# Low parts of weight tiles in a hybrid decoder layer: ScalarE and an accumulating DMA in place of VectorE

## Chip, cores and metric

The kernel runs on one core of one Trainium2 chip. The metric is the device time of one execution in microseconds (us); lower is better. A core has TensorE (matmuls; PE), VectorE (DVE), ScalarE (ACT), GpSimd (POOL) and SyncE (SP), each with a queue of its own that it works through in order, and 16 DMA engines that all queues share.

## What is computed

The reference is one decoder layer over 512 tokens of width 1024 in float32, with a final norm:

```python
u = rmsnorm(x, ln1_g)
q, k, v, pool_in, z, xbc, dt_raw, gate_pre = split(u @ w_in)
y_a = dilated_attention(q, k, v) @ w_a        # 3 groups of 6 heads
y_b = pool_mixer(pool_in, pool_w) @ w_b       # windows 2, 4, 8, 16
y_c = ssd(z, conv(xbc), dt_raw) @ w_c         # chunked scan, 4 chunks of 128
x = x + (sigmoid(gate_pre) * (y_a, y_b, y_c)).sum() @ w_o
x = x + (silu(conv(u2 @ w_up)[:2816]) * conv(u2 @ w_up)[2816:]) @ w_down
out = rmsnorm(x)
```

## The kernel before

**Matmuls in three products.** Each large matrix product is made of operands in a rounded 32-bit format (`F32R`). Both sides are split into a high part (the value rounded to F32R) and a low part (the value minus its high part), and `mm3` (L215 to L222) adds up three products in PSUM: high weight by high activation, high weight by low activation, low weight by high activation, in this order. So the low part of a weight tile is first read after two thirds of a chunk's matmuls.

**Weight tiles as jobs.** The weights pass through 94 jobs, one for each tile; most tiles are 1 MB (128 partitions x 2048 values). A job has three buffers to fill: `raw` (pool `wraw`, two buffers) by a DMA on SP's queue (`fetch`, L168 to L175), `wh` (three buffers) by a rounding copy on ScalarE (`cast`, L177 to L195, two halves of a tile, one for each step), and `wl` (two buffers) by a subtraction on VectorE (`low`, L197 to L210, one instruction for a tile). The loop at L1274 walks through the jobs. Ahead of the matmuls of job n it calls `prepare` (L1281 to L1292): the low part of tile n+1, the high part of tile n+2, the fetch of tile n+3. The fetch needs the raw buffer that the low part of tile n+1 has just finished with.

**The order of the work.** The order on PE, ACT, DVE and POOL is the order in which the program is written (L104); SP's order is chosen by the scheduler. A job of two 128-row chunks calls `step` after each chunk (L143), which first emits one deferred piece of work (`second`, emptied by `flush`, L137) and then one stage of each running side task: attention heads, state-space chunks, norms. Pieces that are left when a job ends are all emitted before the next one begins (L1278).

**Stages.** In order of time: projection to the pooling branch (8 chunks; POOL does its shifted sums, L621 to L643), gates, pooling output, w_b, then for three attention groups v, q and k; the convolution input xbc; the state-space chunks (`ssd_item`, L759) beside the third group and the first gates; z and the last gates; the combination of the three attention groups (`combine`, L576: POOL multiplies attention outputs by weights that SP loads); w_a, w_c, w_o (8 jobs of half the usual number of matmuls, L936), up-projection (22 jobs, `up_evac` L998), down-projection (12 jobs), final norm. Activations and side tasks use one pool of 2 KB tiles (`big`, `NBIG` = 54 buffers, L98 and L1305), handed out in rotation.

Of the kernel before, what the change touches and what calls it, by code (L numbers as in the profile page):

```python
# [11 lines left out]
F32R = mybir.dt.float32r  # L12
AF = mybir.ActivationFunctionType
OP = mybir.AluOpType
AX = mybir.AxisListType

P = 128
# [64 lines left out]
def trunk(ctx: ExitStack, tc, out, x, rel_bias, ln1_g, w_in, b_gate, w_a, pool_w, pool_scale, w_b,  # L82
# [3 lines left out]
    act, dve, pool, pe, sp = nc.scalar, nc.vector, nc.gpsimd, nc.tensor, nc.sync  # L86
# [6 lines left out]
    rows = ctx.enter_context(tc.tile_pool(name="rows", bufs=1))  # L93
    wraw = ctx.enter_context(tc.tile_pool(name="wraw", bufs=2))
    whp = ctx.enter_context(tc.tile_pool(name="whp", bufs=3))
    wlp = ctx.enter_context(tc.tile_pool(name="wlp", bufs=2))
    upool = ctx.enter_context(tc.tile_pool(name="upool", bufs=1))
    big = ctx.enter_context(tc.tile_pool(name="big", bufs=NBIG))  # L98
    ypool = ctx.enter_context(tc.tile_pool(name="ypool", bufs=2))
# [35 lines left out]
    second = []  # L135

    def flush():  # L137
        todo = second[:]
        second.clear()
        for f in todo:  # L140
            f()
# [26 lines left out]
    def fetch(job, cuts=1):  # L168
        raw = job.raw = wraw.tile([P, job.k, job.c], F32, name="raw", tag="raw")
        at = 0  # L170
        for src in job.parts:
            n = src.shape[-1] // cuts
            for i in range(cuts):
                sp.dma_start(raw[:, :, at:at + n], src[:, :, i * n:(i + 1) * n])
                at += n  # L175

    def cast(job, cuts=1, spread=False):  # L177

        w = job.c // cuts
        job.high = whp.tile([P, job.k, job.c], F32R, name="wh", tag="wh")  # L180

        def high(i):
            o = slice(i * w, (i + 1) * w)
            act.copy(job.high[:, :, o], job.raw[:, :, o])  # L184

        def at(i):
            high(i)
            if i + 1 < cuts:
                second.append(lambda: at(i + 1))

        if spread:
            second.append(lambda: at(0))
            return
        for i in range(cuts):
            high(i)  # L195

    def lows(job, cuts=1, eng=None):  # L197

        w, h = job.c // cuts, job.high
        l = wlp.tile([P, job.k, job.c], F32R, name="wl", tag="wl")  # L200
        job.split = h, l
        for i in range(cuts):
            o = slice(i * w, (i + 1) * w)
            (eng or dve).tensor_tensor(l[:, :, o], job.raw[:, :, o], h[:, :, o].bitcast(F32),  # L204
                                       OP.subtract)
            yield

    def low(job, cuts=1, eng=None):
        for _ in lows(job, cuts, eng):
            pass  # L210
# [926 lines left out]
    weights = [j for j in jobs if isinstance(j, Job)]  # L1137
# [87 lines left out]
    pe.transpose(first[2][:, :KD], g8[:KD, :P], eye[:KD, :KD])  # L1225
    dve.tensor_copy(g1, first[2][:, :KD])
    cast(weights[0], 2)
    low(weights[0], 2, pool)
    for k in range(KD):
        turn_scale(1, k % 2 * 4 + k // 2)  # L1230
    for k in range(KD):
        turned(k, 0, bank(k))
    cast(weights[1], 2)
    parts = lows(weights[1], 2)

# [28 lines left out]
    fetch(weights[3])  # L1264
    begin(0, 256, S)
    cast(weights[2])
    low(weights[2])
    begin(1, 256, S)
# [4 lines left out]
    n = 0  # L1273
    for job in jobs:  # L1274
        if not isinstance(job, Job):
            job.fn()
            continue
        while second:  # L1278
            flush()
        if n >= 2:  # L1280
            def prepare(n=n, later=False):  # L1281

                def rest():
                    if n + 1 < len(weights):
                        low(weights[n + 1])
                    if n + 2 < len(weights):
                        cast(weights[n + 2], 2, spread=not later)
                    if n + 3 < len(weights):
                        fetch(weights[n + 3])
                if later:  # L1290
                    return rest
                rest()  # L1292

            if job.late:
                job.prepare = prepare
            else:
                prepare()
            job.body(job.split)
        n += 1
# [2 lines left out]

# [1 line left out]
ORDERED = {EngineType.PE, EngineType.Activation, EngineType.DVE, EngineType.Pool}  # L1304
NBIG = 54  # L1305
MIX = "ZZ0zz1ggggaa"
SSD_ORDER = ((0, 0, 1), (1, 0, 1), (0, 1, 1), (2, 0, 1), (1, 1, 1), (3, 0, 1), (2, 1, 1), (3, 1, 1))
WARM = 12
# [29 lines left out]
```

## Time and profile before

| | us |
|---|---|
| median of 3 runs (1057.33 to 1058.59) | 1057.51 |
| profiled execution, its own time | 1058.24 |
| span of that profile | 1056.4 |
| TensorE busy | 1044.1 |
| VectorE busy, of it L204 (low parts) | 576.7, 219.2 |
| ScalarE busy, of it L184 (high parts) | 430.9, 187.2 |
| GpSimd busy | 134.9 |

The share of busy time is an average over all stages. The DMA engines are busy for 35.9% of the span with the traffic of SP's queue, and move 109 GB/s in the mean. The 1.8 us between the span and the execution's own time lie around the span.

### The profile page before, as it was taken

Reading aid. Unit: us, or ns where it says so; the run is one execution under the profiler, and the core shown is the slowest. Engines: PE = TensorE matmul, PEld = TensorE weight load, DVE = VectorE, ACT = ScalarE, POOL = GpSimd, SP = SyncE. Lnnn points to the kernel's source line nnn. Section 1 sums busy time; section 2 is a strip of 40 time slices with the busy share of each in tenths; the row PEclk is TensorE's granted clock in tenths of the full one; section 3 lists DMA queues with packets and bytes.
Section 4 is the critical chain, followed back from the end, with each engine's and each line's share of the span. In section 5 each row is a group of like instructions: output and inputs, shape, how many; then the busy total and the mean of one; then the engine's idle time right before and its main releaser. Section 6 shows DMA issues by size and latency. Waiting matters only on the chain.

```text
span 1056.4 us, 13018 instructions
## 1 busy us (share of the span) xinstructions
PE 1044.1 (99%) x5268; PEld 872.5 (83%) x5268; DVE 576.7 (55%) x777; ACT 430.9 (41%) x698; POOL 134.9 (13%) x118
## 2 busy tenths in 40 slices
PE   8999999999999999999999999999999999999997
PEld 8878889898788887787888888898888888888885
DVE  5552523245667538576658756766556565532315
ACT  6343412232545633567555323554444434431311
POOL 1580000000000001100143500002111111110100
PEclk9999999999999999999999999999999999999999
DMA  7236233242221355542252426542322323232312
GB/s 241 77 116 180 80 102 94 86 124 67 83 80 60 81 152 137 150 126 57 69 150 83 157 80 217 184 141 80 117 83 94 105 81 120 80 120 77 103 60 80
DMA packets 116426, 115.50 MB, mean 109 GB/s; under 512 B 5235, under 2 KB 101302, under 8 KB 116367
## 3 DMA queue, kind: packets, MB, share of 16 engines
q1 hardware_dynamic: 116367, 114.68, 35.9%
q8 instruction: 41, 0.67, 0.3%
q14 instruction: 18, 0.15, 0.0%
HBM read 110.87 MB, written 2.22 MB: 107 GB/s over the span
## 4 chain that ended last, share of the span: by engine, by line
PE 91%; DMA 2%; issue 2%; ACT 1%; DVE 1%; SPq 1%; POOL 0%; DVEq 0%; ACTq 0%; POOLq 0%
PE pa L221 35%; PE pu L221 22%; PE pb L221 19%; PE pqk L221 7%; DMA al<-ad 1%; PE ps L512 1%; PE pu L1036 1%; PE ppw L221 1%; PE po L551 1%; PE pt L539 1%; DVE wl L204 1%; DMA raw<-in_w_in_dram 1%; SPq L468 1%; PE py L808 1%; PE pyo L814 1%
## 5 line engine op out<-in xcount | busy, mean ns | idle before, releaser
L204 DVE TENSOR_TENSOR wl<-raw,wh 128x2048 fp32r<-128x2048 f32 (+3 forms) x94 | 219.2, 2333 | 137.9 <-PE pb L221 67.6
L184 ACT CAST wh<-raw 128x1024 fp32r<-128x1024 f32 (+2 forms) x186 | 187.2, 1025 | 104.4 <-PE pb L221 41.0
L221 PE MATMUL pa<-uh,wh 128*128 128x512 f32 x384 | 99.3, 400 | 0.3 <-ACT wh L184 0.3
L1003 DVE SCALAR_TENSOR_TENSOR hc<-pu,fcol,hc 128x510 f32<-128x510 f32 x88 | 65.9, 749 | 54.5 <-ACT hc L1000 52.8
L221 PE MATMUL pa<-ul,wh 128*128 128x512 f32 x384 | 95.0, 389 | 0.0
L221 PE MATMUL pa<-uh,wl 128*128 128x512 f32 x384 | 94.9, 389 | 0.0
L221 PEld LDWEIGHTS pa<-ul,wh 128*128 128x128 f32 x384 | 72.1, 188 | 15.3
L221 PEld LDWEIGHTS pa<-uh,wl 128*128 128x128 f32 x384 | 72.1, 188 | 14.9
L221 PE MATMUL pu<-uh,wh 128*128 128x512 f32 (+1 forms) x352 | 83.7, 380 | 0.0
L221 PEld LDWEIGHTS pa<-uh,wh 128*128 128x128 f32 x384 | 69.9, 188 | 16.5 <-issue 1.7
L221 PE MATMUL pu<-ul,wh 128*128 128x512 f32 (+1 forms) x352 | 83.5, 379 | 0.0
L221 PE MATMUL pu<-uh,wl 128*128 128x512 f32 (+1 forms) x352 | 83.5, 379 | 0.0
L221 PEld LDWEIGHTS pu<-ul,wh 128*128 128x128 f32 x352 | 64.2, 188 | 12.5
L221 PEld LDWEIGHTS pu<-uh,wl 128*128 128x128 f32 x352 | 64.2, 188 | 12.4
L221 PEld LDWEIGHTS pu<-uh,wh 128*128 128x128 f32 x352 | 64.1, 188 | 12.5
L1000 ACT ACTIVATE hc<-pu,fcol,fcol 128x512 f32<-128x512 f32 x40 | 31.2, 780 | 82.1 <-PE pu L221 82.1
L1008 POOL TENSOR_TENSOR hc<-hc 128x512 f32<-128x512 f32 x22 | 31.5, 1433 | 223.3 <-DVE hc L1003 188.2
L787 POOL TENSOR_TENSOR xd<-xc,dec 128x512 f32<-128x512 f32 x6 | 6.4, 1063 | 362.9 <-DVE xc L778 344.3
L533 ACT ACTIVATE sb<-sb,nm 128x128 f32<-128x128 f32 (+1 forms) x72 | 30.1, 419 | 47.0 <-DVE nm L530 33.3
L221 PE MATMUL pb<-wh,fl 128*128 128x512 f32 x176 | 47.7, 389 | 0.0
L221 PE MATMUL pb<-wl,fh 128*128 128x512 f32 x176 | 47.7, 389 | 0.0
L221 PE MATMUL pb<-wh,fh 128*128 128x512 f32 x176 | 47.7, 389 | 0.0
(273 smaller groups left out, 1597.6 us busy)
## 6 DMA issues: line engine op xcount, KB each, us to landing
raw<-in_w_in_dram SPq DMA_DIRECT2D x25, 1024.0 KB
raw<-in_ffn_w_up_dram SPq DMA_DIRECT2D x22, 1024.0 KB
raw<-in_w_in_dram SPq DMA_DIRECT2D x20, 512.0 KB
raw<-in_ffn_w_down_dram SPq DMA_DIRECT2D x10, 1024.0 KB
raw<-in_w_o_dram SPq DMA_DIRECT2D x8, 1024.0 KB
raw<-in_w_in_dram SPq DMA_DIRECT2D x6, 768.0 KB
raw<-in_w_b_dram SPq DMA_DIRECT2D x4, 1024.0 KB
al<-ad SPq DMA_DIRECT2D x16, 256.0 KB
```

The costliest lines, as they stand in the source:

```text
L184: act.copy(job.high[:, :, o], job.raw[:, :, o])
L204: (eng or dve).tensor_tensor(l[:, :, o], job.raw[:, :, o], h[:, :, o].bitcast(F32), OP.subtract)
L221: pe.matmul(ps, l, r, start=first and n == 0, stop=last and n == total - 1)
L468: sp.dma_start(V[g, n][32 * tb:32 * tb + 32, :384], t[n:P:4, :384])
L512: pe.matmul(pss[i][:, o:o + w * P], q[r, n * P:(n + 1) * P], k[r, kb * P:(kb + w) * P], start=True, stop=True)
L533: act.activation(sb[:, off:off + w * P], sb[:, off:off + w * P], AF.Exp, bias=nm[:, n, h:h + 1], accum_out=ls[:, n, h:h + 1])
L539: pe.transpose(pt[:, o:o + P], sb[:, o:o + P], eye)
L551: pe.matmul(po[DH * hh:DH * hh + DH, n * P:(n + 1) * P], V[g, kb + i][:, (2 * c + hh) * DH:(2 * c + hh + 1) * DH], probs[2 * c + hh, nb][: ...
L808: pe.matmul(py[DH * i:DH * i + DH, j * P:(j + 1) * P], xc[:, o:o + DH], als[j // 2][:, lo:lo + P], start=True, stop=True)
L1000: act.activation(t, ps, AF.Identity, bias=ff["c1"][:, ff["b"] + m:ff["b"] + m + 1], scale=fw(2, m))
L1003: dve.scalar_tensor_tensor(t[:, sh:], ps[:, :S - sh], fw(k, m), t[:, sh:], OP.mult, OP.add)
L1008: pool.tensor_tensor(a, a, t, OP.mult)
```

## The change

Tiles 4 to 93 get their low part in another way; tiles 0 to 3 keep the old one. The new function `divide` makes four ScalarE pieces: two halves of the high part as before, and two halves of `wl`, written as the raw value times -1 and rounded to F32R, which is the negative of the high part. A DMA on POOL's queue then adds the whole raw tile to `wl` in place. `prepare` calls it for tile n+2 at job n (the low part was made for tile n+1). `wl` gets a third buffer, and the pool of 2 KB tiles shrinks from 54 to 50. Below line 194 the changed kernel's lines are 28 higher than those used here.

```diff
-    wlp = ctx.enter_context(tc.tile_pool(name="wlp", bufs=2))
+    wlp = ctx.enter_context(tc.tile_pool(name="wlp", bufs=3))
...
+    def divide(job, spread=False):
+        w = job.c // 2
+        h = whp.tile([P, job.k, job.c], F32R, name="wh", tag="wh")
+        l = wlp.tile([P, job.k, job.c], F32R, name="wl", tag="wl")
+        job.split = h, l
+        o = [slice(i * w, (i + 1) * w) for i in range(2)]
+        def add():
+            act.mul(l[:, :, o[1]], job.raw[:, :, o[1]], -1.0)
+            pool.dma_start(l, job.raw, accum_op=OP.add)
+        pieces = [lambda: act.copy(h[:, :, o[0]], job.raw[:, :, o[0]]),
+                  lambda: act.copy(h[:, :, o[1]], job.raw[:, :, o[1]]),
+                  lambda: act.mul(l[:, :, o[0]], job.raw[:, :, o[0]], -1.0), add]
+        def at(i):
+            pieces[i]()
+            if i < 3:
+                second.append(lambda: at(i + 1))
+        if spread:
+            second.append(lambda: at(0))
+        else:
+            for f in pieces:
+                f()
...
-                    if n + 1 < len(weights):
-                        low(weights[n + 1])
+                    if n == 2:
+                        low(weights[3])
                     if n + 2 < len(weights):
-                        cast(weights[n + 2], 2, spread=not later)
+                        divide(weights[n + 2], spread=not later)
                     if n + 3 < len(weights):
                         fetch(weights[n + 3])
...
-NBIG = 54
+NBIG = 50
```

## Prediction

> **What bounds the kernel now.** I read the page's busy times, then who PE waited for, then PE's stretches along the span, then the queues that feed PE's weight tiles.
>
> ```profile
> span 1056.4 us, 13018 instructions
> ...
> PE 1044.1 (99%) x5268; PEld 872.5 (83%) x5268; DVE 576.7 (55%) x777; ACT 430.9 (41%) x698; POOL 134.9 (13%) x118
> ...
> PE 91%; DMA 2%; issue 2%; ACT 1%; DVE 1%; SPq 1%; POOL 0%; DVEq 0%; ACTq 0%; POOLq 0%
> ...
> L204 DVE TENSOR_TENSOR wl<-raw,wh 128x2048 fp32r<-128x2048 f32 (+3 forms) x94 | 219.2, 2333 | 137.9 <-PE pb L221 67.6
> L184 ACT CAST wh<-raw 128x1024 fp32r<-128x1024 f32 (+2 forms) x186 | 187.2, 1025 | 104.4 <-PE pb L221 41.0
> ```
>
> TensorE is busy for 99% of the span; VectorE, which the change relieves, for 55%. The list of PE's waits says what could be won:
>
> ```profile
> PE pcb L782 <- DVE ea L816: 1.0, 1, 1.0
> PE pbt L753 <- ACT o L557: 0.4, 1, 0.4
> ...
> PE pa L221 <- ACT wh L184: 0.3, 1, 0.3
> ```
>
> (us in total, times, longest.) From 38 us on to the last matmul these three, 1.7 us, are all. The first follows a low part: DVE ran L204 until 410.2 and only then the L816 that PE waited for. The 219.2 us of L204 lie beside matmuls and cost nothing else. So the question is not what VectorE saves, but whether the new way delivers each tile in time.
>
> **What is removed and added.** 90 of the 94 low parts leave DVE (90 x about 2.3 us). 180 ScalarE pieces come, priced as the high halves at L184: 1.03 us for a half of a 1 MB tile, some 187 us in all, so ACT goes from 431 to about 618 us (58%). 90 DMAs come on POOL's queue, each waiting for ACT's last piece; behind a waiting one stand POOL's products. Each fetch on SP waits for such a DMA to land instead of for L204 (SP waits 799.3 us for L204 now, so it always waits); behind it on SP stand the loads of the state-space chunks (L766) and of the combination (L602).
>
> **The unknown: A**, from the issue of an accumulating DMA to its landing. The trace has none. The nearest row is a fetch of the same size. One is issued at 708.39; columns: stretch, length, the busy time of five engines, clock, DMA share, GB/s:
>
> ```profile
> 708.00:709.00 1.00, 1.00 (x11) 1.00 (x10) 0.97 (x2) 0.16 (x1) 0.00 (x0) 1.00 0.07 16
> 709.00:710.00 1.00, 1.00 (x10) 1.00 (x10) 0.75 (x1) 0.14 (x1) 0.00 (x0) 1.00 0.40 53
> 710.00:711.00 1.00, 1.00 (x11) 1.00 (x10) 0.00 (x0) 1.00 (x2) 0.00 (x0) 1.00 0.99 318
> 711.00:712.00 1.00, 1.00 (x9) 0.96 (x8) 0.00 (x0) 1.00 (x2) 0.00 (x0) 1.00 1.06 370
> 712.00:713.00 1.00, 1.00 (x6) 0.79 (x6) 0.83 (x2) 1.00 (x3) 0.00 (x0) 1.00 0.88 297
> 713.00:714.00 1.00, 1.00 (x6) 0.84 (x5) 0.92 (x2) 0.72 (x2) 0.16 (x1) 1.00 0.03 10
> ```
>
> It is over at 713.1: F = 4.7 us. An addition reads two tiles and writes one where a fetch reads one and writes one. Ends: 4.7 (as a fetch) and 14.1 (three passes, each as a fetch). I take 1.5 times F, by the bytes: A = 7.1, an estimate. The Trainium skill (Collectives: The Full Stack, "Why ReduceScatter is half of AllGather") says that an added element needs two source reads on one ring and so goes at half the copy's rate; with the fit of 2.0 us + bytes/436e3 for a DMA issued by GpSimd (DMA: Bandwidth & Descriptors, "Anatomy of one DMA") that would be an estimate of 6.8 us, and the sum below would be 2 us less. No row here shows it.
>
> **Place 1, the first tiles: +2.4 us.** POOL is full of the pooling branch's sums when the first DMAs come:
>
> ```profile
> 59.02 2.97 POOL L629 TENSOR_TENSOR psw<-psw 128x508 f32<-128x508 f32 x1
> ...
> 65.78 1.03 POOL L629 TENSOR_TENSOR psw<-psw 128x508 f32<-128x508 f32 x1
> ...
> 72.08 2.97 POOL L629 TENSOR_TENSOR psw<-psw 128x508 f32<-128x508 f32 x1
> ...
> 76.74 0.22 POOL L632 TENSOR_TENSOR psw<-psw,ramp 128x16 f32<-128x16 f32 x1
> ```
>
> In the changed order the DMA of tile 4 stands after the sixth chunk's sums (now done at 62.4), that of tile 5 after the eighth's (77.0). Three sums (49.13, 59.02, 72.08) ran beside a low part and took 2.7 to 3.0 us instead of 1.04; without it they give back 5.4. So tile 5's DMA goes out at 77.0 - 5.4 + 0.8 for the two issues = 72.4 and lands at 79.5. PE reads that low part from 77.06. Tile 4 is 1.7 late (58.9 + 7.1 against 64.34), which is part of the same 2.4.
>
> **Place 2, the combination: +3.0 us.** The DMA of the third gate tile stands behind the sixth product with wb, now done at 559.7 (557.6 without its collision with a low part): 557.6 + 7.1 = 564.7, against 561.66.
>
> **Place 3, w_o: +18.9 us.** Here a job is 24 matmuls, 5.45 us, not 10.9:
>
> ```profile
> 640.00:686.00 46.00, 46.00 (x212) 38.09 (x212) 31.69 (x45) 23.84 (x38) 5.18 (x4) 1.00 0.60 200
> ```
>
> PE never stops in it now. A raw buffer serves every second tile, so its round has to fit into 10.9 us (two jobs): fetch 4.7 + four pieces 4.2 + A 7.1 = 16.0. ScalarE's pieces of w_o's second tile end at about 645.7 (three pieces after the cast at 642.23), its low part lands at 652.8, and PE reads it from 647.77: 5.0 late. Tiles 4, 6, 8 and the second up tile follow at 16.0 each; PE reads them now at 658.65, 671.30, 682.71 and 697.89, and each is 5.1, 3.4, 4.6 and 0.8 later than PE's own delay so far. The sum is 18.9.
>
> **Elsewhere: nothing.** In stages of 10.9 us a job the round has 21.8 us. A row of the up-projection is the tightest:
>
> ```profile
> 723.03 0.78 ACT L1000 ACTIVATE hc<-pu,fcol,fcol 128x512 f32<-128x512 f32 x1
> 725.47 0.63 ACT L1005 ACTIVATE hc<-hc 128x512 f32<-128x512 f32 x1 [1.66 <-DVE hc L1003]
> 726.00 1.03 ACT L184 CAST wh<-raw 128x1024 fp32r<-128x1024 f32 x1
> ```
>
> After a chunk, ACT scales, waits for DVE, applies silu; three pieces follow and the DMA goes out some 6.5 us after the chunk's last matmul. PE wants the low part one job and eight plus eight matmuls later, at 14.5: A up to 8.0 is hidden. In the state-space stage the change from 54 to 50 buffers delays writers: set against these times, POOL's st product at 440.3 gets a buffer that PE reads until 453.3, DVE's score add at 432.5 one read until 438.2. Behind the first stands tile 37's DMA: 454.4 + 7.1 = 461.5, against 467.1 when PE reads it. The cover is 5.6 us; DVE's 5.7 us are covered by the L204 that leaves there (2.28) and by idle 3.25 before 439.37. I count 0, and -1.0 for the PE wait behind L204.
>
> **Sum:** 2.4 + 3.0 + 18.9 - 1.0 = +23.3, on this execution's 1058.24 (0.7 above the median): 1081.5, I say 1082. At A = 4.7: 0 + 0.6 + 8.5 - 1.0 = +8.1 (1066). At A = 11: 6.3 + 6.9 + 38.4 - 1.0, and 3.0 for each of ten pairs of up jobs: +81 (1139). At 14.1 every stage's round (23.0) is over its two jobs: +200.
>
> **Rivals.**
> - *The forecast's mechanism with A from 4.7 to 9* (w_o's round over 10.9): 0.57.
> - *A above 9*: every a-half of the up-projection is late, then the gates: 1100 to 1139 up to A = 11, far more beyond. For it: two reads, a cast to F32R, POOL writing the descriptors, fetches on the same engines (share 0.60 in w_o). Against: engines idle 64% of the time. 0.28. Within it, POOL held up by DVE: POOL's 1.04 us became 2.97 beside L204. If descriptors suffer so, A is 9.0 where DVE is busy: +1.0 for ten pairs, some +11 in w_o, +2 each in the other places, about 1107. The Trainium skill (DMA: Bandwidth & Descriptors, "SWDGE vs HWDGE vs iDMA") says as much: GpSimd writes descriptors into SBUF state from which DVE can lock it out; no row shows it for descriptors. 0.10 of the 0.28.
> - *SP and POOL blocked in the state-space stage*: loads at L766 stand behind fetches that now go out 2 to 7 us later, st products behind the 50 buffers. +5 to +15, near 1092: 0.06.
> - *Not slower*: the addition lands within 2.0 us, for then w_o's second tile comes by 647.7, before PE reads it, and the round (10.9) fits. The three waits go: -1.7, about 1056.5. Against it: F alone is 4.7. 0.09, of it 0.04 for a gain over 0.2% (2.1 us, about what a measurement of this kernel can tell from no change).
>
> **Range and chances.** The likeliest is 1082. From 1060 to 1150 takes in A from about 4 to 11.5; the rest, some 0.08 below and 0.11 above, is left out. Slower 0.91, same 0.05, faster 0.04.
>
> **What would show it.** Right: PE waits for the accumulating DMA at L221 between 640 and 700 for about 19 us in steps of 3 to 5, 2 to 3 us near 65 to 80 and near 562; L204 gone from DVE; ACT near 618 us. Wrong: such waits in every up job (A over 8), or waits on DVE and ACT between 420 and 490, or none at all.

## The result and the profile after

The changed kernel takes **1150.82 us** (median of 4 runs, 1147.13 to 1152.96); the kernel before takes 1057.42 us beside it. The ratio is 1.0879 (95% interval 1.0845 to 1.0914). The forecast had the sign and most of the places, but a quarter of the size: +24 of +93 us. The profiled execution took 1149.12 us. Five lines of its page, and then who PE waited for (us in total, times, longest). The line numbers in a view are those of the kernel that it was taken from:

```profile
span 1147.0 us, 13439 instructions
...
PE 1066.1 (93%) x5268; PEld 882.0 (77%) x5268; DVE 370.4 (32%) x687; ACT 597.4 (52%) x878; POOL 201.0 (18%) x208
...
PEclk9979999999999979999999998788999999999999
...
q0 software_dynamic: 12960, 91.30, 40.2%
...
wl<-raw POOLq DMA_DIRECT2D x80, 1024.0 KB, 7.9
```

```profile
PE pb L249 <- DMA wl<-raw: 35.6, 8, 10.1
PE pa L249 <- DMA wl<-raw: 15.4, 5, 5.2
PE pqk L249 <- DMA wl<-raw: 13.2, 1, 13.2
PE pu L1064 <- DMA wl<-raw: 4.2, 1, 4.2
```

VectorE is relieved by 206 us, and it does not matter. PE, hardly idle before, waits 68.4 us in these four rows and 69.3 with two small ones, always for the accumulating DMA. A tile of 1 MB lands 7.9 us after its issue (all 90: 4.5 to 11.9, median 7.7), so the guess for A (7.1) is near the median, but A is not one number. The clock row shows something that was not in the forecast at all: slices with a granted clock of 0.7 and 0.8.

Both kernels issue the same 5268 matmuls in the same order. So the start of each matmul in one trace minus its start in the other says exactly where time was lost. In the table this is done for every kernel below (without the extra matmuls of `fill`); the stretches are those of the kernel before, in us.

| kernel | to 40 | first tiles, 40-100 | 100-340 | third group and state-space, 340-520 | combination, 520-620 | w_o and first up jobs, 620-720 | up and down, 720-end | sum |
|---|---|---|---|---|---|---|---|---|
| forecast | 0 | 2.4 | 0 | -1.0 | 3.0 | 18.9 | 0 | 23.3 |
| changed | -0.9 | 9.9 | 1.0 | 21.0 | 11.9 | 45.5 | 2.6 | 90.9 |
| up_down | 1.4 | 0.0 | 0.0 | 10.6 | 0.0 | 0.9 | 4.4 | 17.4 |
| no_wo | 1.5 | 9.8 | 2.4 | 21.8 | 9.9 | 2.4 | 5.3 | 53.1 |
| add_dram | 0.1 | 9.7 | 0.5 | 19.1 | 11.1 | 69.1 | 2.0 | 111.5 |
| copy | -0.1 | 2.1 | 0.0 | 12.3 | 2.9 | 23.9 | 0.0 | 41.1 |
| fill | -1.1 | 10.6 | 2.0 | 20.2 | 12.2 | 47.0 | 4.8 | 95.7 |
| alt_wo | 1.4 | 0.0 | 0.0 | 10.6 | 0.0 | 35.9 | 0.0 | 47.9 |
| b50 | 1.1 | 0.0 | 0.0 | 11.5 | 0.0 | -0.2 | 0.0 | 12.5 |
| two_steps | -0.4 | 10.8 | 7.4 | 12.9 | 8.8 | 43.3 | 1.9 | 84.5 |
| neg_dve | -0.7 | 8.9 | 3.0 | 15.9 | 7.6 | 35.0 | 2.3 | 72.0 |
| places | -0.3 | 0.0 | 0.0 | 5.1 | 0.0 | 0.8 | 3.8 | 9.4 |

The first column differs by 2.6 us between kernels that are alike there; it varies from one execution to the next.

**w_o.** PE's stretches in the changed kernel; columns: stretch, length, busy PE, weight loads, DVE, ACT, POOL, then clock, DMA share, GB/s.

```profile
698.00:700.00 2.00, 0.00 (x0) 0.00 (x0) 0.00 (x0) 0.00 (x0) 0.00 (x0) 0.50 1.03 236
...
706.00:708.00 2.00, 2.00 (x10) 1.69 (x9) 0.69 (x1) 0.63 (x2) 0.58 (x1) 1.00 1.03 398
708.00:710.00 2.00, 2.00 (x10) 1.65 (x9) 0.15 (x1) 0.09 (x2) 0.71 (x1) 1.00 0.88 249
710.00:712.00 2.00, 2.00 (x10) 1.35 (x8) 0.00 (x0) 1.78 (x2) 0.00 (x0) 1.00 0.90 348
712.00:714.00 2.00, 1.77 (x9) 1.43 (x8) 0.00 (x0) 2.00 (x3) 0.00 (x0) 1.00 0.02 7
714.00:716.00 2.00, 0.38 (x2) 0.00 (x0) 0.00 (x0) 2.00 (x4) 0.88 (x1) 1.00 0.10 20
716.00:718.00 2.00, 0.00 (x0) 0.00 (x0) 0.00 (x0) 1.91 (x3) 0.00 (x0) 1.00 1.14 229
```

From 701 to 721 us the 16 DMA engines are full for some 16 us, and idle for 4 (712 to 716) while ScalarE makes the pieces of two tiles. One raw buffer's round, from the instruction starts and landings of the trace: fetch issued at 701.15, landed at 710.12 (9.0 us); four pieces to 714.13; the addition issued at 714.53 and landed at 721.55 (7.0); the next fetch at 721.62. That is 20.5 us for two jobs whose matmuls need 10.9.

The first of w_o's waits is not such a round. SyncE's queue, GpSimd's queue and then PE there (start, length, instruction, idle before and its releaser):

```profile
685.84 5.57 SPq L962 DMA_DIRECT2D x<-in_x_dram  x8
```

```profile
689.30 0.86 POOL L208 DMA_DIRECT2D wl<-raw  x1 [10.08 <-ACT wl L207]
695.41 0.86 POOL L208 DMA_DIRECT2D wl<-raw  x1 [5.25 <-ACT wl L207]
```

```profile
701.23 2.05 PE L249 MATMUL pb<-wl,mgh 128*128 128x512 f32 x4 [10.10 <-DMA wl<-raw]
```

The addition of 689.30 landed at 701.10, after 11.8 us and not 7: beside it ran a fetch, eight loads of x (2 MB in all) and, from 695.41, the next tile's addition. PE loses 10.3 us there. From this wait's end to the end of the fifth (783.73) four rounds take 82.5 us, 20.6 each, where the kernel before needs 50.1 us: 32.4 are lost. Together that is 42.7 of the 45.5 us.

**The longest wait**, 13.2 us, is in the third attention group, where the forecast had nothing. The timelines of ScalarE, then GpSimd, then PE there (start, length, instruction, idle before and its releaser):

```profile
394.63 1.05 ACT L211 CAST wh<-raw 128x1024 fp32r<-128x1024 f32 x1 [0.89 <-DMA raw<-in_w_in_dram]
401.53 1.28 ACT L822 ACT_TABLE_LOAD   x1 [5.85 <-DMA al<-ad]
...
405.27 1.04 ACT L212 ACTIVATE wl<-raw 128x1024 fp32r<-128x1024 f32 x1
406.22 1.04 ACT L207 ACTIVATE wl<-raw 128x1024 fp32r<-128x1024 f32 x1
```

```profile
407.67 0.87 POOL L208 DMA_DIRECT2D wl<-raw  x1 [20.48 <-ACT wl L207]
```

```profile
418.15 3.44 PE L249 MATMUL pqk<-uh,wl 128*128 128x512 f32 x8 [13.21 <-DMA wl<-raw]
```

The high halves of tile 32 are done at 395.7, but its negative halves come at 405.3: between them in ScalarE's order stands the exp of a state-space chunk (L822), idle until its loads land (L794). SP issued these at 396.4, behind a fetch into the raw buffer whose addition had landed only at 392.1. So the DMA goes out 10 us late and, with loads beside it, takes 10.4.

### The profile page after: what moved, and what is told of

The parts are those of the page before. It is cut to its first block, busy times and chain, and to the rows that moved or that the text cites. A ratio compares the mean times of both kernels' runs of the same rounds, so it can differ in the third digit from the quotient of the medians.

```text
span 1147.0 us, 13439 instructions
## 1 busy us (share of the span) xinstructions
PE 1066.1 (93%) x5268; PEld 882.0 (77%) x5268; DVE 370.4 (32%) x687; ACT 597.4 (52%) x878; POOL 201.0 (18%) x208
## 3 DMA queue, kind: packets, MB, share of 16 engines
q0 software_dynamic: 12960, 91.30, 40.2%
q1 hardware_dynamic: 116367, 114.68, 32.7%
## 4 chain that ended last, share of the span: by engine, by line
PE 51%; DMA 24%; issue 17%; ACT 3%; POOL 2%; DVE 2%; SPq 0%; POOLq 0%; DVEq 0%; ACTq 0%
PE pu L249 18%; DMA wl<-raw 14%; PE pa L249 14%; PE pb L249 9%; PE pqk L249 6%; DMA raw<-in_w_o_dram 3%; DMA raw<-in_w_in_dram 2%; DMA raw<-in_ffn_w_down_dram 1%; POOL psw L657 1%; DMA raw<-in_w_c_dram 1%; PE ppw L249 1%; DMA raw<-in_ffn_w_up_dram 1%; PE py L836 1%; DMA al<-ad 1%; PE ps L540 1%
## 5 line engine op out<-in xcount | busy, mean ns | idle before, releaser
L208 POOL DMA_DIRECT2D wl<-raw x90 | 78.5, 872 | 728.3 <-ACT wl L207 668.4
L210 ACT CAST wh<-raw 128x1024 fp32r<-128x1024 f32 (+2 forms) x90 | 91.4, 1015 | 143.2 <-DMA raw<-in_ffn_w_down_dram 51.2
L249 PE MATMUL pa<-uh,wl 128*128 128x512 f32 x384 | 98.8, 401 | 14.6 <-DMA wl<-raw 14.6
L212 ACT ACTIVATE wl<-raw 128x1024 fp32r<-128x1024 f32 (+2 forms) x90 | 92.3, 1026 | 0.0
L211 ACT CAST wh<-raw 128x1024 fp32r<-128x1024 f32 (+2 forms) x90 | 91.1, 1013 | 0.9 <-DMA raw<-in_w_in_dram 0.9
L207 ACT ACTIVATE wl<-raw 128x1024 fp32r<-128x1024 f32 (+2 forms) x90 | 91.6, 1017 | 0.0
L249 PEld LDWEIGHTS pu<-uh,wh 128*128 128x128 f32 x352 | 64.9, 191 | 12.5
L249 PEld LDWEIGHTS pu<-ul,wh 128*128 128x128 f32 x352 | 64.6, 190 | 12.5
L249 PEld LDWEIGHTS pu<-uh,wl 128*128 128x128 f32 x352 | 64.0, 188 | 13.2 <-issue 0.6
L249 PE MATMUL pb<-wl,mgh 128*128 128x512 f32 x64 | 21.1, 459 | 30.6 <-DMA wl<-raw 30.6
L249 PE MATMUL pqk<-uh,wl 128*128 128x512 f32 x144 | 37.0, 401 | 13.2 <-DMA wl<-raw 13.2
```

The source lines that it names most:

```text
L207: act.mul(l[:, :, o[1]], job.raw[:, :, o[1]], -1.0)
L208: pool.dma_start(l, job.raw, accum_op=OP.add)
L210: pieces = [lambda: act.copy(h[:, :, o[0]], job.raw[:, :, o[0]]), lambda: act.copy(h[:, :, o[1]], job.raw[:, :, o[1]]), lambda: act.mul(l[ ...
L211: lambda: act.copy(h[:, :, o[1]], job.raw[:, :, o[1]]),
L212: lambda: act.mul(l[:, :, o[0]], job.raw[:, :, o[0]], -1.0), add]
L249: pe.matmul(ps, l, r, start=first and n == 0, stop=last and n == total - 1)
```

## The experiments

Theory to test first: fetch and addition share the DMA engines and ScalarE's order makes additions late, place by place. Rivals: lateness is inherited from tile to tile; the smaller pool costs by itself; A is long because of the path and not the addition; the slow clock is the loss.

**up_down: only tiles 62 to 93 by the DMA.** A predicate `by_dma(m)` chooses between the two ways:

```diff
-                    if n == 2:
-                        low(weights[3])
+                    if n + 1 < len(weights) and not by_dma(n + 1):
+                        low(weights[n + 1])
                     if n + 2 < len(weights):
-                        divide(weights[n + 2], spread=not later)
+                        if by_dma(n + 2):
+                            divide(weights[n + 2], spread=not later)
+                        else:
+                            cast(weights[n + 2], 2, spread=not later)
...
+    def by_dma(m):
+        return m >= 62
```

> Only tiles 62 to 93 (up- and down-projection) get their low part from ScalarE and the DMA; all others from VectorE as before, with the changed kernel's three low and 50 big buffers. If the loss sits where PE's matmuls fell behind (from the second up job to the end only 3.5 of 90.9 us): 1060 to 1061 us, and no delay before 700 us. Rival, the buffers or the new order cost something in the state-space stage by themselves (there the changed kernel lost 20.6 us): 1068 to 1080, with the delay between 360 and 480 us.

Measured: 1075.07 us, ratio 1.0182 (1.0165 to 1.0199). The projections lose 5.3 us, a little more than expected, but 10.6 are lost in a stage where no tile uses the DMA. The rival held for it: the buffers have a price of their own.

**b50: the pool alone.**

```diff
-NBIG = 54
+NBIG = 50
```

> The kernel before with 50 big buffers in place of 54, nothing else. If the smaller pool is what the up- and down-projection run lost between 420 and 500 us: 10 to 11 us there, and 1067 to 1069 us. Rival, the third low buffer or the transition does it: 1057 to 1059 us.

Measured: 1067.96 us, ratio 1.0105 (1.0088 to 1.0121); 11.5 us lost from 340 to 520, nothing elsewhere. Two rows of PE's waits in this kernel:

```profile
PE pxs L776 <- DVE ea L816: 4.1, 2, 2.3
...
PE pcb L782 <- DVE ea L816: 2.5, 2, 1.9
```

PE waits for VectorE's L816, which the forecast's wait list showed once, with 1.0 us. In the changed kernel VectorE has no low parts in this stretch, and from 340 to 530 us PE waits for nothing but the accumulating DMA.

**no_wo: w_o by VectorE.** The same predicate, `4 <= m < 52 or m >= 62`.

> Tiles 52 to 61 (w_o and the first two up tiles) get their low part from VectorE, all others as in the changed kernel. If w_o is a place of its own: its 44.5 us go, 1150.8 - 44.5 = 1106 us, the delay up to 640 us stays at 43. Rival, w_o only collects a lateness that the queues bring along: 1115 to 1130, with waits moved to the first tiles after it.

Measured: 1110.66 us, ratio 1.0528 (1.0484 to 1.0571). w_o loses 2.4 us and the stages ahead of it about as much as in the changed kernel. It is a place of its own.

**copy: the addition left out.**

```diff
-            pool.dma_start(l, job.raw, accum_op=OP.add)
+            pool.dma_start(l, job.raw)
```

> As the changed kernel, but the DMA copies the raw tile over the low buffer and does not add; the addition is left out. If the addition makes the transfer long (two reads for one write): issue to landing falls from 7.7 to about 5, w_o's round by 3 to 6 us, 1100 to 1115 us. Rival, a transfer of 1 MB from SBUF to SBUF through GpSimd's queue takes this long with or without an addition: 7 to 8 us, 1145 to 1155 us.

Measured: 1101.86 us, ratio 1.0437 (1.0419 to 1.0454). The queue's row and the time to landing in this kernel's page:

```profile
q0 software_dynamic: 12960, 91.30, 22.4%
...
wl<-raw POOLq DMA_DIRECT2D x80, 1024.0 KB, 4.3
```

The same bytes and packets: with the addition 7.9 us to landing and 40.2% of the engines over 1147.0 us (461 us), without it 4.3 us and 22.4% over 1097.2 (246 us). The addition makes each DMA occupy the engines 1.88 times as long. More than half of the loss hangs on it (49 of 93 us); the rest stays without it.

**add_dram: w_o's addition reads DRAM.** The raw buffer is then free after the pieces.

```diff
-            pool.dma_start(l, job.raw, accum_op=OP.add)
+            if job in weights[52:60]:
+                for k in (0, 2):
+                    pool.dma_start(l[:, k:k + 2, :], job.parts[0][:, k:k + 2, :], accum_op=OP.add)
+            else:
+                pool.dma_start(l, job.raw, accum_op=OP.add)
```

> As the changed kernel, but for the eight w_o tiles the addition reads the weights from DRAM again (two DMAs of half a tile) and not the raw buffer, which is so free after ScalarE's last piece. Theory of the raw buffer's round (fetch 9.0, pieces 4.2, addition 7.0, one after the other, 20.5 us for two jobs): the round becomes 13.3, w_o loses 4.5 x (13.3 - 10.9) = 11 instead of 44.5 us, 1117 us. Theory of the shared DMA engines (share 0.80 to 0.94 in w_o; packets' time about 5.3 us of all 16 engines for an addition and 3.4 for a fetch, so 17.4 us for two tiles): w_o still loses 4.5 x (17.4 - 10.9) = 29 us, 1135 us.

Measured: 1174.43 us, ratio 1.1109 (1.108 to 1.1139): slower than either theory. The edit brought a bound of its own. In the trace each half of a tile goes out only when the half before has landed (landings at 697.34 and 703.61, the next issues at 697.68 and 703.95) and takes 6.0 us in the median, so a tile costs 12. It tells nothing between the two theories.

**alt_wo: every second tile of w_o.** The predicate `52 <= m < 62 and m % 2 == 1`.

> Only the even tiles of w_o and the second up tile (53, 55, 57, 59, 61) get their low part from ScalarE and the DMA, all others from VectorE; 50 big and three low buffers. Such a tile's raw buffer still has a round of fetch 4.7, pieces 4.2 and addition 7.0 in two jobs of 10.9, but half of the additions are gone. If the round without contention is what makes w_o late, as the forecast had it: w_o loses 4 to 5 us for each pair, 18 to 20. If the full DMA engines do: two fetches and one addition need about 11 us of engines in 10.9, w_o loses 0 to 4. In both cases 10 to 11 us are lost between 420 and 500 us, as in the run with the up- and down-projection alone. So 1086 to 1088 against 1068 to 1072 us.

Measured: 1105.74 us, ratio 1.0458 (1.0442 to 1.0473); w_o loses 35.9 us. Both theories are off: half of the additions keep four fifths of the loss. Three stretches of this kernel (columns as above):

```profile
660.00:662.00 2.00, 0.00 (x0) 0.00 (x0) 1.96 (x1) 0.00 (x0) 0.00 (x0) 1.00 0.98 197
662.00:664.00 2.00, 0.00 (x0) 0.00 (x0) 0.00 (x0) 0.00 (x0) 0.00 (x0) 0.62 1.09 197
...
668.00:670.00 2.00, 2.00 (x7) 1.55 (x7) 0.84 (x2) 0.72 (x2) 0.88 (x1) 0.67 1.05 390
```

An addition alone (660 to 662) fills all 16 engines. The other tile's fetch, issued at 661.99, brings no more GB/s until the addition lands at 666.1; then two fetches run together (390 GB/s), and the one issued at 666.1 is there after 6.8 us, not 4.7. That round is 6.8 + 3.9 for the pieces + 0.3 + 7.8 = 18.8 us. w_o's first wait ends at 666.3 and the fifth at 744.6, so four rounds take 78.3 us where the kernel before needs 50.1: 28.2 are lost, and with the first wait's 6.4 that is 34.6 of the 35.9 in the table. So the two theories are one: the buffer's round sets the pace, and its links are as long as the shared engines make them.

**neg_dve: shorter pieces.** Both negative halves go to VectorE:

```diff
-            act.mul(l[:, :, o[1]], job.raw[:, :, o[1]], -1.0)
+            dve.tensor_scalar(l[:, :, o[1]], job.raw[:, :, o[1]], -1.0, None, OP.mult)
...
```

> The changed kernel with the two negative halves on VectorE in place of ScalarE, at the same places of the program. If w_o's loss is the number of its rounds times what a round is longer than two jobs (now fetch 9.0 beside the other tile's addition, pieces 4.2, addition 7.0 and 0.3 between: 20.5 against 10.9), pieces on two engines side by side take some 2.2: the round is 18.5, w_o loses 4.5 x 7.6 = 34 to 36 instead of 44.5 us. Job 32's wait stays, since VectorE too stands behind an operation (L821) that waits for the same loads: 1140 to 1143 us. Rival, the engines of the DMA alone set w_o (16 us of a round are full): they fill the gap, w_o loses 42 to 45 us and the time stays at 1149 to 1152 us.

Measured: 1131.22 us, ratio 1.0712 (1.0688 to 1.0736). w_o loses 35.0 us, as expected, and its rounds are near the 18.5 us expected: the first two take 18.6 and 19.2 us from fetch to fetch, all four 75.3 in place of 82.5. That the expected sum (4.5 equal losses) hits the total is partly luck: the first wait costs 9.7 us and the four rounds lose 25.2. The DMA engines alone do not set w_o. The time is 9 us better than expected, for the third group and the combination gain too. One row of PE's waits:

```profile
PE pqk L249 <- DMA wl<-raw: 9.1, 1, 9.1
```

Job 32's wait is 4 us shorter; that it would stay was wrong.

**two_steps: ScalarE's order.**

```diff
             pieces[i]()
-            if i < 3:
-                second.append(lambda: at(i + 1))
+            pieces[i + 1]()
+            if i < 2:
+                second.append(lambda: at(i + 2))
```

> The changed kernel with the four ScalarE pieces of a tile in two steps (high half and negative half together) and not in up to four. In job 32's tile ScalarE had its high halves at 395.7 us, but wrote the negative halves at 405.3, behind an exp that waited for loads of the state-space chunk. If this order makes the 13.4 us wait: the DMA goes out some 9 us earlier, the wait is 3 to 6 us, 1140 to 1143 us, and w_o is as before (its pieces already follow one another). Rival, the transfers are late by contention: the wait stays at 10 to 13 us, 1147 to 1152 us.

Measured: 1142.49 us, ratio 1.0832 (1.0787 to 1.0877). ScalarE's timeline in this kernel, and a row of PE's waits:

```profile
395.58 1.06 ACT L212 ACTIVATE wl<-raw 128x1024 fp32r<-128x1024 f32 x1
...
409.36 1.28 ACT L823 ACT_TABLE_LOAD   x1 [11.77 <-DMA al<-ad]
```

```profile
PE pqk L250 <- DMA wl<-raw: 4.0, 1, 4.0
```

Tile 32's negative halves now stand ahead of the exp; its DMA goes out at 398.0, lands at 408.6, and PE, which reads it at 410.2, does not wait. The wait of 4.0 is the next tile's (33), whose four pieces now stand behind that exp; its DMA goes out at 417.4. So the order on ScalarE made the long wait, and PE loses 8 us less in that stretch. The new order has a price of its own: 6.4 us more between 100 and 340, where PE now waits 4.2 us for the pooling weight.

**fill: PE kept busy in the waits.** The slow clock tested: extra matmuls, whose result nobody reads, ahead of the third product.

```diff
         for a, b in ((wh, xh), (wh, xl), (wl, xh)):
+            if a is wl and filler:
+                d = SM("dum")
+                l, r = (xh(ks[0]), wh(ks[0])) if flip else (wh(ks[0]), xh(ks[0]))
+                for _ in range(filler.pop()):
+                    pe.matmul(d[:, :r.shape[-1]], l, r, start=True, stop=True)
...
+FILL = {4: 16, 32: 52, 44: 22, 53: 44, 55: 32, 57: 26, 59: 32}
```

> The changed kernel, with extra matmuls of one high tile by one high activation, whose result nobody reads, ahead of the third product where PE waited longest: 16, 52 and 22 in jobs 4, 32 and 44 and 44, 32, 26 and 32 in w_o's jobs 2, 4, 6 and 8, each set a little shorter than the wait it fills. If PE's own idleness halves the granted clock: no matmuls at 427 ns after these waits; the first tiles lose 4 to 5 instead of 9.9 us, job 32 and job 44 1.4 less each; w_o still loses 44 to 45, since there the transfers set the time and not PE; 1150.8 - 8 = 1143 us. Rival, the slow matmuls come from the transfers beside them: they stay, 1149 to 1152 us.

Measured: 1154.02 us, ratio 1.0922 (1.0903 to 1.0941). The ten us after the first stall in the changed kernel, and then in this one (columns as above):

```profile
70.00:80.00 10.00, 10.00 (x26) 5.83 (x25) 2.61 (x5) 4.54 (x6) 3.85 (x7) 0.51 0.74 182
```

```profile
70.00:80.00 10.00, 10.00 (x46) 7.86 (x45) 2.48 (x5) 7.52 (x9) 3.75 (x7) 1.00 0.71 171
```

The clock stays at 1.00 and 46 matmuls pass instead of 26: PE's own idleness had halved it. But the time does not fall. Tile 7's low part lands at 106.9 us here and at 106.5 in the changed kernel, whether PE comes early or late, and here PE waits for it:

```profile
106.99 3.75 PE L255 MATMUL pa<-uh,wl 128*128 128x512 f32 x8 [3.70 <-DMA wl<-raw]
```

Both expectations were wrong: the slow clock is real and costs next to nothing here, since the transfers set the pace and the slow matmuls only take the place of a wait. In two of the seven places the extra matmuls ended after the addition had landed, by 1.4 and 0.9 us; that is too little to hide the 8 us that were expected.

**places: the DMA's way where it was not late.** Pieces in two steps, the predicate `9 <= m < 29 or 38 <= m < 42 or m >= 62`.

> The pieces in two steps, and VectorE's way for the tiles where the DMA's way came late (4 to 8, 29 to 37, 42 to 61); the DMA's way for the 47 others (9 to 28, 38 to 41, 62 to 93). If the places add up: nothing lost up to 400 us, 10 to 12 us from 420 to 500 for the 50 big buffers while VectorE has its subtractions there, 2 to 4 us in the up- and down-projection: 1070 to 1073 us. Rival, each lateness was inherited from the tile ahead and moves to the next: 1080 to 1100 us.

Measured: 1068.59 us, ratio 1.0107 (1.0092 to 1.0122). The places add up: nothing is lost up to 400 us, in the state-space stage 5.1 us, half of what was expected, and no lateness moved on to the next tile. Of b50's four waits behind L816 two are left; the two after 470 us of the kernel before, where tiles 38 to 41 go by the DMA, are gone. With 56 tiles moved off VectorE (56 additions in the trace; the expectation's 47 is a miscount) this is still slower than the kernel before; no version here beats it.

## Why the prediction was wrong, point by point

- **The bound, and what could be won: right.** PE was the bound and nearly nothing could be gained; the wait behind L204 did go (-1.2 us between 400 and 420, forecast -1.0).
- **A = 7.1: near the median, in part by luck** (7.0 in w_o's round, median 7.7). The reason given, 1.5 times a fetch by the bytes, is not what copy shows: a plain copy lands after 4.3 us and the addition makes it 7.9, a factor of 1.84. Nor is A one number: for a tile of 1 MB it went from 6.9 to 11.9 us. The stated range ended at 1150, which was to need an A of 11.5; the time came there with a median A of 7.7. The Trainium skill's rule (Collectives: The Full Stack, "Why ReduceScatter is half of AllGather"), that an added element needs two reads and so goes at half the rate, agrees with the 1.88 of copy.
- **Place 3, w_o, +18.9, measured 45.5: the mechanism right, the sizes off; this term failed most.** The step that failed is the sum fetch 4.7 + four pieces 4.2 + A 7.1 = 16.0: it priced each transfer as if it ran alone. The fetch's 4.7 came from a row in which no other transfer ran; beside additions that fill the engines it took 9.0, and the round 20.5. The forecast's four rounds are 64.0 us and lose 13.9 against the 50.1 of the kernel before; they took 82.5 and lost 32.4. The first addition of w_o went out when the forecast said (689.30; 645.7 moved by 43.2 us of delay is 688.9), but landed after 11.8 us, so the first wait costs 10.3 us and not 5.0. The rest of the 45.5 is mostly slow matmuls behind the last wait. A bound would have warned of it: an addition holds all 16 engines for 461/90 = 5.1 us (1.5 times a fetch would have said the same) and a fetch for about 3.3 (35.9% of 1056.4 us for 114.68 MB before), which makes 17 us of engines for two tiles, in 10.9. With engines that full, times of quiet transfers do not hold.
- **Place 1, +2.4, measured 9.9.** Both issue times were right to about a microsecond (59.98 and 73.56, forecast 58.9 and 72.4), and so was the cause, POOL's sums. What failed is to stop there: tiles 6 and 7 fetch into the raw buffers that these late additions free, and are late next. In the changed kernel this lateness is spent on slow matmuls (4.1 of the 9.9 us are the wait for tile 4), in fill on the wait for tile 7. copy, with its shorter transfers, loses 2.1.
- **Place 2, +3.0, measured 11.9.** PE waits twice, 3.3 and 5.2 us, where the forecast had one wait, and matmuls are slow behind the second. The second gate tile's addition took 8.7 us. The third gate tile's DMA went out at 594.45; 557.6 moved by the delay so far (30.9) is 588.5. The products ahead of it waited for wb loads, which stood on SP behind a fetch that waited for an addition, with the engines at 0.93 (575 to 585). SyncE's queue, then GpSimd's, there:

```profile
583.25 0.40 SPq L174 DMA_DIRECT2D raw<-in_w_in_dram  x1
583.69 7.88 SPq L630 DMA_DIRECT2D wb<-wd  x11
```

```profile
589.82 4.68 POOL L632 TENSOR_TENSOR o<-o,wb 128x512 f32<-128x512 f32 x3 [2.50 <-DMA wb<-wd]
594.45 0.86 POOL L208 DMA_DIRECT2D wl<-raw  x1
```

- **Elsewhere 0: wrong by 22 us in the third group and the state-space stage.** The forecast looked at POOL's queue and at buffers. It missed that the negative halves are steps of their own on ScalarE, behind an exp whose loads stand on SP behind a late fetch. The rival "SP and POOL blocked in the state-space stage" had half of this, at 0.06 and at 5 to 15 us.
- **The rival of POOL held up by DVE** does not show where it could be seen: the 90 issues on POOL's queue took 0.85 to 1.03 us each, and none was stretched as the sums were.
- **50 buffers: right as far as the runs go.** The delays are there (11.5 us in b50). Where VectorE's low parts go they are covered: the changed kernel has none of these waits, places has two of four, and neg_dve, where VectorE has the negative halves, has them again, but shorter.
- **Up- and down-projection: nearly right**, 2.6 us with A at 7.9, where the cover was put at 8.0.
- **What would show it:** waits in w_o, near 63 and near 580 and 596 came, in w_o 6 to 10 us each and not 3 to 5. Waits in every up job, or on DVE and ACT between 420 and 490, did not come. ScalarE came to 597 us, forecast 618.

Not settled: how much of w_o a third raw buffer would win back. It would take the room of four more 2 KB buffers (1 MB is 8 KB a partition) and was not tried.

## What to carry to other kernels

Price every link of a buffer's round at what the shared DMA engines leave it, and add up the engines' time for a stage's transfers before trusting a chain of quiet durations. A new step on an in-order engine must be placed against every instruction there that may wait for a load; look at which load that is and what stands ahead of it on its queue. When a tile is late, ask which buffer it frees late: the next loss in that stage is there.

## What the runs showed of the hardware

- An accumulating DMA of 1 MB fills all 16 DMA engines alone and holds them 1.88 times as long as a copy; in alt_wo a fetch issued in its middle brought no more GB/s until it had landed, and in the changed kernel's w_o a fetch beside an addition took 9.0 us instead of 4.7.
- PE's granted clock halves soon after PE stops, and matmuls take 427 instead of 227 ns from start to start. In the longest wait PE's last matmul starts at 404.56; the clock is 1.00 to 407 us and 0.50 then:

```profile
408.00:418.00 10.00, 0.00 (x0) 0.00 (x0) 2.52 (x8) 4.77 (x6) 2.49 (x3) 0.50 0.90 172
418.00:421.00 3.00, 2.85 (x7) 2.29 (x8) 0.00 (x0) 0.00 (x0) 0.00 (x0) 0.50 1.01 199
421.00:423.00 2.00, 2.00 (x20) 1.31 (x19) 0.33 (x2) 0.60 (x1) 0.00 (x0) 0.98 0.96 124
```

  It is full again 2.9 us after PE resumes at 418.15. That is not always so soon: behind the first stall PE resumes at 67.55, and the clock is 0.51 from 70 to 80 us. In the changed kernel waits of 3.3 us and less left no such matmuls, waits of 3.9 and more did; in up_down waits of 2.3 and 1.8 us with a few short matmuls behind them did too. The Trainium skill (TensorE: Matmul & The Clock Gate, "Part 1: The HAM clock gate") says that a window of 3.4 us without work halves the clock and one of work restores it; the rows of the longest wait agree in size, those of the first stall and of up_down do not fit so simply. What it cost depends on who sets the pace: fill shows that here it was the transfers.
